# Sums of weight quarters for the seven products: from VectorE to accumulating DMAs

## Chip, cores and metric

The kernel runs on one core of one Trainium2 chip. The metric is the device time of one execution, in microseconds (us). Times come from one execution taken by the hardware profiler and from three timed runs.

## What is computed

One inference step of a backbone of two layers, on 640 tokens (128 context, 512 latent) of 1024 channels, in float32. Every layer is an FFN, a group of mixers (two attentions, a recurrence, a retention), and another FFN. The FFNs matter here; their hidden width is 2816, which is 22 chunks of 128:

```
def swiglu(h, wg, wu, wd):
    return (jax.nn.silu(h @ wg) * (h @ wu)) @ wd
...
  x += 1/2 * gate1 * SwiGLU_1(adaLN_1(RMSNorm(x)))
  x += gate2 * W_out [A | B | C | D](adaLN_2(RMSNorm(x)) @ W_in)
  x += 1/2 * gate3 * SwiGLU_2(adaLN_3(RMSNorm(x)))
```

## The kernel before

Channels lie on the 128 partitions, tokens along the free axis. Every float32 operand is split in two parts, high and low, and a product is made of three matmuls on TensorE (PE): high by high, high by low, low by high (`mm3`, L271 to L275). For weights, `parts` (L159) lets ScalarE (ACT) copy the high part (L168) and VectorE (DVE) subtract it for the low one (L169).

A hidden chunk needs a gate product and an up product. The first chunks of an FFN (`PLAIN`: 5, 4, 4 and 3 of the 22) are done plainly. The other 72 chunks of the four FFNs go through `strassen` (L593): the two weight blocks of a chunk, gate = [A11 | A12] and up = [A21 | A22], are taken as one 2 by 2 matrix of 512-column quarters, the activations as another one, and gate and up come out of seven products instead of eight (Winograd's form). A product is four `mm3`, so 12 matmuls of 320 columns, and a chunk is 84. Its accumulators are X, Y and Z in PSUM; `finish` (L602) copies or adds them after each product.

The seven weight operands are A11, S1 = A21 + A22, S2 = S1 - A11, S4 = A12 - S2, S3 = A11 - A21, A12 and A22. `seven` (L201) lists them as seven items. It loads gate and up whole (512 KB each); the four sums are made by DVE (L215, L219, L224, L228) in tiles named `ws`, and then split like any weight.

What sets the order: `take(ahead, deep)` (L177) hands out the next item to the program. When an item is used, those up to `AHEAD` = 2 items later are made (summed and split), and those up to `DEEP` = 7 further on are loaded. All loads are issued by SP, in that order, into a pool of 15 tiles of 128 x 1024 (`wide`) that loaded, summed and split weights share; a load waits until its tile is free. Each engine does its instructions in the order in which the program's scheduler put them. The 22 chunks are done in parts of four or three (`PARTS`, L17); after each part `down` (L678) multiplies the part's hidden chunks by eight weight tiles, one product of 24 or 18 matmuls each, and adds them to x on DVE (L682). Among the chunks of three of the four FFNs DVE also does rows of the modulation (L318, `mod_row`), with weights of 512 KB each. GpSimd (POOL) makes sums of the activations (`sums`, L460) before the first seven-product chunk of an FFN and small work of the mixers; it issues no DMA.

The sum S1, for example, is added before the split:

```
def s1():
    st["u"] = u = tiles.pop(r)
    st["s"] = wide("ws")
    V.tensor_add(st["s"][:, :512], u[:, :512], u[:, 512:])
    return parts(st["s"][:, :512], 512)
```

Of the kernel before, what the change touches and what calls it, by code (L numbers as in the profile page):

```python
# [53 lines left out]
def trunk(tc, A, O):  # L54
# [3 lines left out]
    with ExitStack() as es:  # L58
# [17 lines left out]
        def other():  # L76
            """the end of the stack of pools changes its form between the FFNs and the mixers"""
# [40 lines left out]
        # ---------------------------------------------------------------- constants, residual, conditions  # L118
# [18 lines left out]
        # ---------------------------------------------------------------- weights, prefetched in order  # L137
# [7 lines left out]
        def fetch(upto):  # L145
            while state["raw"] <= min(upto, len(raws) - 1):
                i = state["raw"]
                ap, n = raws[i]
# [6 lines left out]
                D.dma_start(out=dst, in_=ap)  # L155
                tiles[i] = raw
                state["raw"] += 1

        def parts(src, n):  # L159
            """the two parts of a float32 operand"""  # L160
# [6 lines left out]
            def go():  # L167
                S.activation(hi, src, AF.Copy)  # L168
# [8 lines left out]
        def take(ahead=2, deep=0):  # L177
            """the next weights; those of the next `ahead` items are made, the next `deep` of them loaded"""
# [10 lines left out]
        def plain(ap, n):  # L189
            raws.append((ap, n))  # L190
# [3 lines left out]
        def halved(ap, n):  # L194
            """a load of two items"""
            raws.append((ap, 2 * n))
# [4 lines left out]
        def seven(gate, up):  # L201
            """the weights of the seven products of one hidden chunk: gate = [A11 | A12], up = [A21 | A22]"""
            raws.append((gate, 1024))
            raws.append((up, 1024))
# [3 lines left out]
            def a11():  # L208
                st["g"] = tiles.pop(r - 1)
                return parts(st["g"][:, :512], 512)  # L210

            def s1():
                st["u"] = u = tiles.pop(r)
                st["s"] = wide("ws")
                V.tensor_add(st["s"][:, :512], u[:, :512], u[:, 512:])  # L215
                return parts(st["s"][:, :512], 512)

            def s2():
                V.tensor_sub(st["s"][:, 512:], st["s"][:, :512], st["g"][:, :512])  # L219
                return parts(st["s"][:, 512:], 512)  # L220

            def s4():
                st["s4"] = wide("ws")
                V.tensor_sub(st["s4"][:, :512], st["g"][:, 512:], st["s"][:, 512:])  # L224
                return parts(st["s4"][:, :512], 512)

            def s3():
                V.tensor_sub(st["s4"][:, 512:], st["g"][:, :512], st["u"][:, :512])  # L228
                return parts(st["s4"][:, 512:], 512)
# [26 lines left out]
        def ffn_units(l, w):  # L256
            for k0, k1 in PARTS:
                for f in range(k0, k1):
                    gu = [A["wgu"][l, w, f, i] for i in range(2)]
                    if f < PLAIN[l][w]:  # L260
                        for ap in gu:
                            plain(ap, 1024)
                    else:
                        seven(*gu)
# [6 lines left out]
        def mm3(out, wh, wl, xh, xl, first, last, more=False):  # L271
            """out (+)= w x, three products of their parts; `more` goes on with sums that were read already"""
# [11 lines left out]
        # ---------------------------------------------------------------- modulation  # L284
        # per (layer, group): tile [128, 2 conditions (latent, context), 8 chunks]
# [24 lines left out]
        def mod_row(l, g, k, c):  # L310
            """one condition's products for 128 columns of w_mod"""
# [417 lines left out]
        C = {}  # L729
# [793 lines left out]
```

## Time and profile before

| | |
|---|---|
| median of three runs | 2520.91 us (2519.56 to 2529.28) |
| profiled execution, span | 2521.9 us (the page gives no other time of it) |
| PE busy | 2467.4 us, 98% |
| DVE busy | 1974.8 us, 78% |
| ACT busy | 1141.8 us, 45% |
| POOL busy | 244.8 us, 10% |
| DMA | 261.88 MB, mean 104 GB/s |

An engine's busy time is the union of its instructions. A matmul is shown for some 310 ns but the next one begins 0.15 us after it, so that PE's pace is its busy time over the number of its matmuls. Idle time of an engine is put down to the instruction or DMA that ended it. The granted clock is that of PE; 1.00 is 2.4 GHz.

### The profile page before, as it was taken

To read this page: it belongs to the slowest core of one execution; us is meant where nothing else is said; L and a number is where in the kernel's file an instruction comes from. 1 tells how busy PE (TensorE), PEld (TensorE's weight loads), DVE (VectorE), ACT (ScalarE), POOL (GpSimd) and SP (SyncE) were. 2 spreads that over 40 slices of the span, in tenths; PEclk is the share of its full clock that TensorE was granted. 3 is DMA by queue.
4 is the path that set the end of the run, shared out by engine and by line. 5 is a ranking of instruction groups with operands and counts; after the bars stand their busy time and mean duration, and the time that the engine had idled before them with its cause. 6 is when DMAs were issued, how large, how long until landed. Compare 5 with 4: busy or idle time off the path is not lost.

```text
span 2521.9 us, 43865 instructions
## 1 busy us (share of the span) xinstructions
PE 2467.4 (98%) x17376; PEld 2365.6 (94%) x17376; DVE 1974.8 (78%) x3850; ACT 1141.8 (45%) x2271; POOL 244.8 (10%) x251
## 2 busy tenths in 40 slices
PE   7999999999999999999999999999999999999999
PEld 6999999996888999999999999999878789999999
DVE  6899989856666898988989898897656668666765
ACT  5344334563345633443463344344634556433433
POOL 2100000022420200000020000000433102000000
PEclk9999999999999999999999999999999999999999
DMA  7544344222102244443424444342110022222222
GB/s 253 185 152 138 127 129 148 94 78 67 37 18 66 93 144 134 143 133 118 141 89 148 134 142 133 119 134 78 58 60 26 18 76 76 77 67 81 87 81 71
DMA packets 92303, 261.88 MB, mean 104 GB/s; under 512 B 10049, under 2 KB 20929, under 8 KB 92097
## 3 DMA queue, kind: packets, MB, share of 16 engines
q1 hardware_dynamic: 92096, 259.07, 31.7%
q8 instruction: 137, 2.24, 0.4%
q14 instruction: 70, 0.57, 0.1%
HBM read 255.63 MB, written 3.41 MB: 103 GB/s over the span
## 4 chain that ended last, share of the span: by engine, by line
PE 67%; DVE 4%; ACT 2%; POOL 1%; issue 1%; DVEq 0%; POOLq 0%; ACTq 0%
PE dn L273 8%; PE dn L274 7%; PE dn L275 7%; PE x L274 5%; PE x L275 5%; PE x L273 5%; PE y L274 3%; PE y L275 3%; PE y L273 3%; PE pt L1290 2%; PE ao L1299 2%; PE g L274 2%; PE g L273 2%; PE g L275 1%; PE z L273 1%; PE z L274 1%
## 5 line engine op out<-in xcount | busy, mean ns | idle before, releaser
L273 PE MATMUL dn<-hidh,wp 128*128 128x320 f32 x1408 | 434.5, 311 | 0.0
L275 PE MATMUL dn<-hidh,wp 128*128 128x320 f32 x1408 | 433.9, 309 | 0.0
L274 PE MATMUL dn<-hidl,wp 128*128 128x320 f32 x1408 | 433.7, 309 | 0.2 <-DVE hidl L281 0.2
L168 ACT ACTIVATE wp<-ws 128x512 fp32r<-128x512 f32 x288 | 180.8, 630 | 393.2 <-DVE ws L215 149.9
L168 ACT ACTIVATE wp<-raw 128x512 fp32r<-128x512 f32 (+1 forms) x408 | 243.7, 611 | 212.1 <-DVE wp L169 84.2
L682 DVE SCALAR_TENSOR_TENSOR x<-dn,mod,x 128x128 f32<-128x128 f32 (+3 forms) x488 | 233.8, 518 | 126.4 <-PE dn L275 125.3
L318 DVE SCALAR_TENSOR_TENSOR junk<-wm,cond 128x1024 bf16<-128x1024 f32 x256 | 304.5, 1218 | 4.6 <-DMA wm<-in_wmod 4.5
L169 DVE TENSOR_TENSOR wp<-raw,wp 128x512 fp32r<-128x512 f32 (+1 forms) x408 | 266.2, 667 | 51.9 <-ACT wp L168 47.0
L273 PEld LDWEIGHTS dn<-hidh,wp 128*128 128x128 f32 x1408 | 264.5, 188 | 4.8 <-ACT hidh L280 3.7
L274 PEld LDWEIGHTS dn<-hidl,wp 128*128 128x128 f32 x1408 | 264.8, 188 | 0.6 <-DVE hidl L281 0.6
L275 PEld LDWEIGHTS dn<-hidh,wp 128*128 128x128 f32 x1408 | 264.6, 188 | 0.0
L169 DVE TENSOR_TENSOR wp<-ws,wp 128x512 fp32r<-128x512 f32 x288 | 197.4, 691 | 17.6 <-ACT wp L168 17.0
L274 PE MATMUL g<-hl,whi 128*128 128x320 f32 x608 | 192.6, 318 | 3.2 <-DVE hl L528 1.7
L275 PE MATMUL g<-hh,wlo 128*128 128x320 f32 x608 | 190.5, 314 | 0.0
L273 PE MATMUL g<-hh,whi 128*128 128x320 f32 x608 | 185.5, 318 | 4.5 <-ACT hh L527 2.2
L273 PE MATMUL x<-hh,wp 128*128 128x320 f32 x576 | 178.3, 310 | 1.0 <-DVE sl L613 1.0
L274 PE MATMUL x<-hl,wp 128*128 128x320 f32 x576 | 178.5, 310 | 0.0
L275 PE MATMUL x<-hh,wp 128*128 128x320 f32 x576 | 178.3, 309 | 0.0
L169 DVE TENSOR_TENSOR wlo<-raw,whi 128x1024 fp32r<-128x1024 f32 x88 | 109.8, 1249 | 61.2 <-ACT whi L168 46.0
L425 POOL TENSOR_TENSOR nrs<-nrm,neghalf 80x4 f32<-80x4 f32 x12 | 13.3, 1106 | 1377.1 <-DVE nrm L423 1377.1
L168 ACT ACTIVATE whi<-raw 128x1024 fp32r<-128x1024 f32 x88 | 92.5, 1052 | 80.5 <-PE dk L274 20.7
L274 PEld LDWEIGHTS g<-hl,whi 128*128 128x128 f32 x608 | 117.1, 193 | 5.9 <-DVE hl L454 3.5
(331 smaller groups left out, 6655.2 us busy)
## 6 DMA issues: line engine op xcount, KB each, us to landing
raw<-in_wgu SPq DMA_DIRECT2D x176, 512.0 KB, 3.5
wm<-in_wmod SPq DMA_DIRECT2D x128, 512.0 KB, 4.0
raw<-in_wd SPq DMA_DIRECT2D x64, 512.0 KB, 3.8
raw<-in_wd SPq DMA_DIRECT2D x32, 384.0 KB, 3.4
raw<-in_wint SPq DMA_DIRECT2D x20, 512.0 KB, 3.5
wm<-in_wm SPq DMA_DIRECT2D x32, 256.0 KB, 5.5
raw<-in_wqkv SPq DMA_DIRECT2D x16, 512.0 KB, 3.5
raw<-in_wocd SPq DMA_DIRECT2D x8, 512.0 KB, 3.4
```

What stands on the lines that cost most here:

```text
L168: S.activation(hi, src, AF.Copy)
L169: V.tensor_sub(lo, src, hi.bitcast(F32))
L273: PE.matmul(out, wh, xh, start=first, stop=False, skip_group_check=more)
L274: PE.matmul(out, wh, xl, start=False, stop=False, skip_group_check=more)
L275: mark["pe"] = PE.matmul(out, wl, xh, start=False, stop=last, skip_group_check=more)
L318: V.scalar_tensor_tensor(junk, modraw["w"], 1.0, cond[c], OP.mult, OP.mult, accum_out=modraw[(l, g)][:, c, k:k + 1])
L425: G.tensor_tensor(r, s, neghalf[:80, :4], op=OP.pow)
L682: V.scalar_tensor_tensor(x[d][:, s0:s1], pv[:, s0 - base:s1 - base], gate[:, c, d:d + 1], x[d][:, s0:s1], OP.mult, OP.add)
L1290: PE.transpose(p[:, c0 - a0:c0 - a0 + 128], P[:, c0:c0 + 128], idn)
L1299: PE.matmul(o[kv * 64:kv * 64 + 64, :128], vs[i][:, kv * 64:kv * 64 + 64], pts[kv][:, i * 128:i * 128 + 128], start=i == 0, stop=i == nb - 1)
```

## The change

Three sums come from DMAs that add what they read to what the tile holds, issued by POOL. The tile z is loaded as [A11 | A21], and `up` = [A21 | A22] is accumulated on it, so that it holds [A11 + A21 | A21 + A22]. Its right half is S1 with the sign turned; A11 is then accumulated on it (S2 turned), and A12 (S4). Each accumulation waits until the split of the sum before has read the half. So `up` stands with its sign turned in all seven products: S3 = A11 + A21, S1 = -(A21 + A22), S2 = S1 - A11, S4 = A12 - S2. `parts` has a form that splits the negative of its source. A22 is loaded by itself. The up half of a hidden chunk comes out negative; one sum of the activations (L475) changes its sign, the plain chunks take a factor -1 (L665), and the FFN's gate is multiplied by -0.5 instead of 0.5 (L389 of before). The products run in the order X, Y, X, Z, X, Y, X instead of X, Y, X, Y, X, Z, X, and the steps of `finish` move with them.

```
 def fetch(upto):
...
                 D.dma_start(out=dst, in_=ap)
+                if add is not None:
+                    G.dma_start(out=raw[:, :n], in_=add, accum_op=OP.add)
...
+        def parts(src, n, neg=False):
...
+                if neg:
+                    S.activation(hi, src, AF.Copy, scale=-1.0)
+                    V.scalar_tensor_tensor(lo, src, -1.0, hi.bitcast(F32), OP.mult, OP.subtract)
+                    return
...
+        def seven(gu):
+            gate, up = gu[0], gu[1]
+            raws.append((gate, 1024, None))
+            raws.append((gu[:, :, :512].rearrange("i p n -> p i n"), 1024, up))
+            raws.append((up[:, 512:], 512, None))
             r = len(raws) - 1
             st = {}
 
             def a11():
-                st["g"] = tiles.pop(r - 1)
+                st["z"] = z = tiles.pop(r - 1)
+                st["s1"] = parts(z[:, 512:], 512, True)
+                G.dma_start(out=z[:, 512:], in_=gate[:, :512], accum_op=OP.add)
+                st["g"] = tiles.pop(r - 2)
                 return parts(st["g"][:, :512], 512)
...
             def s2():
-                V.tensor_sub(st["s"][:, 512:], st["s"][:, :512], st["g"][:, :512])
-                return parts(st["s"][:, 512:], 512)
+                z = st["z"]
+                p = parts(z[:, 512:], 512, True)
+                G.dma_start(out=z[:, 512:], in_=gate[:, 512:], accum_op=OP.add)
+                return p
...
-            for make in (s1, s2, s4, s3, lambda: parts(st["g"][:, 512:], 512), lambda: parts(st["u"][:, 512:], 512)):
+            for make in (lambda: st.pop("s1"), s2, lambda: parts(st["g"][:, 512:], 512), lambda: parts(st["z"][:, :512], 512),
+                         lambda: parts(st["z"][:, 512:], 512), lambda: parts(tiles.pop(r)[:, :512], 512)):
                 items.append((r, make))
...
-                V.tensor_scalar(o[:, :, k0:k1], o[:, :, k0:k1], 0.5, None, OP.mult)
+                V.tensor_scalar(o[:, :, k0:k1], o[:, :, k0:k1], -0.5, None, OP.mult)
...
-                E1.tensor_sub(t4[:, 320:], hi[:, :320], t[:, 320:])
+                E1.tensor_sub(t4[:, 320:], t[:, 320:], hi[:, :320])
...
                     elif i == 3:
+                        V.tensor_add(ct[:, one], ct[:, one], Z)
+                        S.activation(ct[:, one], ct[:, one], AF.Silu)
+                    elif i == 4:
+                        V.tensor_add(sl[:, two], sl[:, one], X)
+                    elif i == 5:
                         V.tensor_add(ct[:, two], ct[:, two], Y)
                         S.activation(ct[:, two], ct[:, two], AF.Silu)
-                    elif i == 4:
-                        V.tensor_add(sl[:, two], sl[:, one], X)
                         V.tensor_mul(sl[:, two], sl[:, two], ct[:, two])
...
-                for i, (o, b, new) in enumerate(((X, "11", True), (Y, "t1", True), (X, "t2", False), (Y, "22", False),
-                                                 (X, "t3", False), (Z, "21", True), (X, "t4", False))):
+                for i, (o, b, new) in enumerate(((X, "11", True), (Y, "t1", True), (X, "t2", False), (Z, "21", True),
+                                                 (X, "t3", False), (Y, "22", False), (X, "t4", False))):
...
-                    V.tensor_mul(sl, sl, uv)
+                    V.scalar_tensor_tensor(sl, uv, -1.0, sl, OP.mult, OP.mult)
```

The diff also drops comments and moves line numbers by a few: L168 and L169 are L174 and L175 after the change, the negative form is L171 and L172, and the accumulations are L157 (`up` on z), L220 (A11) and L227 (A12).

What stands on DVE before, in the fourth chunk of a part of the first layer's second FFN (raw_17152 is the gate, raw_17173 is up, `wp` the split weights, `junk` the modulation):

```order
L215 TENSOR_TENSOR ws_17308<-raw_17173 128x512
L219 TENSOR_TENSOR ws_17308<-ws_17308,raw_17152 128x512
L281 TENSOR_TENSOR hidl_17191<-sl_17058,hidh_17190 128x640
L169 TENSOR_TENSOR wp_17310<-ws_17308,wp_17310 128x512
L318 SCALAR_TENSOR_TENSOR junk_17256,modraw_16973<-wm_17254,cond_14257 128x1024
L318 SCALAR_TENSOR_TENSOR junk_17313,modraw_16973<-wm_17254,cond_14260 128x1024
L169 TENSOR_TENSOR wp_17338<-ws_17308,wp_17338 128x512
L224 TENSOR_TENSOR ws_17356<-raw_17152,ws_17308 128x512
L228 TENSOR_TENSOR ws_17356<-raw_17152,raw_17173 128x512
```

The same chunk on DVE after the change (raw_17115 is z, raw_17113 the gate; wp_17245 is S1, wp_17293 is S2, wp_17346 is S4):

```order
L172 SCALAR_TENSOR_TENSOR wp_17245<-raw_17115,wp_17245 128x512
L280 TENSOR_TENSOR hidl_17151<-sl_17019,hidh_17150 128x640
L175 TENSOR_TENSOR wp_17249<-raw_17113,wp_17249 128x512
L317 SCALAR_TENSOR_TENSOR junk_17213,modraw_16932<-wm_17211,cond_14222 128x1024
L317 SCALAR_TENSOR_TENSOR junk_17269,modraw_16932<-wm_17211,cond_14225 128x1024
L172 SCALAR_TENSOR_TENSOR wp_17293<-raw_17115,wp_17293 128x512
L175 TENSOR_TENSOR wp_17312<-raw_17113,wp_17312 128x512
L609 TENSOR_TENSOR ct_17157<-ct_17157,z_17156 128x320
L175 TENSOR_TENSOR wp_17328<-raw_17115,wp_17328 128x512
L612 TENSOR_TENSOR sl_17158<-sl_17158,x_17154 128x320
L175 TENSOR_TENSOR wp_17346<-raw_17115,wp_17346 128x512
```

The four sums are gone; between the splits of S1, S2 and S4, each of which reads what a DMA has written since the last, stand the other splits, two rows of the modulation and sums from PSUM.

On POOL nothing stood in these chunks before. After the change, around the third (raw_16976) and fourth chunk (raw_17115) of the same part:

```order
L157 DMA raw_16976<-in_wgu 128x1024
L227 DMA raw_16807<-in_wgu 128x512
L220 DMA raw_16976<-in_wgu 128x512
L157 DMA raw_17115<-in_wgu 128x1024
L227 DMA raw_16976<-in_wgu 128x512
L220 DMA raw_17115<-in_wgu 128x512
L227 DMA raw_17115<-in_wgu 128x512
```

The first accumulation of a chunk comes between the second and the third of the chunk before.

## Rows read from the trace of the kernel before

**Rows 1.** The page's first part: busy time, share, instructions by engine.
```profile
span 2521.9 us, 43865 instructions
...
PE 2467.4 (98%) x17376; PEld 2365.6 (94%) x17376; DVE 1974.8 (78%) x3850; ACT 1141.8 (45%) x2271; POOL 244.8 (10%) x251
```

**Rows 2.** Busy time by engine in the seven-product stretches of the four FFNs.
```profile
core 0: us, PE busy (x) PEld busy (x) DVE busy (x) ACT busy (x) POOL busy (x), PEclk, DMA share, GB/s
140.00:460.00 320.00, 319.05 (x2170) 317.71 (x2169) 295.25 (x573) 138.35 (x259) 2.90 (x1) 1.00 0.43 140
860.00:1240.00 380.00, 379.52 (x2571) 377.83 (x2569) 341.21 (x598) 157.92 (x291) 11.58 (x11) 1.00 0.42 135
1300.00:1680.00 380.00, 379.50 (x2575) 377.90 (x2575) 338.58 (x597) 157.62 (x294) 12.02 (x12) 1.00 0.41 133
2110.00:2500.00 390.00, 389.52 (x2648) 387.94 (x2647) 266.99 (x464) 164.92 (x307) 0.78 (x1) 1.00 0.25 76
sum 1470.00, PE 1467.59 PEld 1461.38 DVE 1242.03 ACT 618.81 POOL 27.28; mean PE 366.90 PEld 365.34 DVE 310.51 ACT 154.70 POOL 6.82
```

**Rows 3.** PE's waits over the whole span: us in total, times, longest.
```profile
PE nsum L421 <- DVE sq L412: 13.1, 1, 13.1
PE ro L1073 <- DVE pm L1067: 8.7, 2, 4.4
...
PE x L273 <- DVE sl L613: 1.0, 2, 0.6
```

**Rows 4.** Groups of DVE instructions by shape: count, busy us, mean ns, idle before.
```profile
L169 DVE TENSOR_TENSOR wp<-ws,wp 128x512 fp32r<-128x512 f32 x288 | 197.4, 691 | 17.6 <-ACT wp L168 17.0
...
L219 DVE TENSOR_TENSOR ws<-ws,raw 128x512 f32<-128x512 f32 x72 | 50.1, 696 | 1.0
L215 DVE TENSOR_TENSOR ws<-raw 128x512 f32<-128x512 f32 x72 | 49.9, 692 | 0.7 <-PE x L275 0.7
L224 DVE TENSOR_TENSOR ws<-raw,ws 128x512 f32<-128x512 f32 x72 | 49.4, 686 | 1.4 <-PE x L275 0.3
L228 DVE TENSOR_TENSOR ws<-raw 128x512 f32<-128x512 f32 x72 | 49.3, 684 | 0.0
...
L616 DVE TENSOR_TENSOR ct<-ct,z 128x320 f32<-128x320 f32 x72 | 34.8, 483 | 4.2 <-PE z L275 3.6
...
L665 DVE TENSOR_TENSOR sl<-sl,g 128x640 f32<-128x640 f32 x16 | 13.0, 815 | 8.8 <-PE g L275 6.7 <-ACT sl L664 2.0
```

**Rows 5.** The group of ACT's high parts of the sums.
```profile
L168 ACT ACTIVATE wp<-ws 128x512 fp32r<-128x512 f32 x288 | 180.8, 630 | 393.2 <-DVE ws L215 149.9 <-PE dn L275 82.8 <-DVE ws L224 54.9
```

**Rows 6.** DMA queues (share of 16 engines) and issues (median us to landing).
```profile
q1 hardware_dynamic: 92096, 259.07, 31.7%
...
raw<-in_wgu SPq DMA_DIRECT2D x176, 512.0 KB, 3.5
...
wm<-in_wm SPq DMA_DIRECT2D x32, 256.0 KB, 5.5
...
ck<-in_ck SPq DMA_DIRECT2D x2, 256.0 KB, 4.0
cv<-in_cv SPq DMA_DIRECT2D x2, 256.0 KB, 2.8
```

**Rows 7.** The groups of POOL instructions: a small tensor operation and the cheapest.
```profile
L425 POOL TENSOR_TENSOR nrs<-nrm,neghalf 80x4 f32<-80x4 f32 x12 | 13.3, 1106 | 1377.1 <-DVE nrm L423 1377.1
...
L880 POOL MEMSET xp<- 128x3 f32 x4 | 0.4, 96 | 0.0
```

**Rows 8.** The tile raw on SP: ns of an issue, and all its landings.
```profile
L155 SPq DMA_DIRECT2D raw<-in_wgu x176: 327/328/1055, 11.4 to 2456.7; - x176
...
DMA to landing us min/median/max: 3.1/3.6/8.3
```

**Rows 9.** Timeline of PE in a mixer: start us, us, instruction, idle time before it.
```profile
585.57 0.74 PE L1073 MATMUL ro<-pm,dvn 128*64 128x512 f32 x1 [4.39 <-DVE pm L1067]
```

**Rows 10.** Busy time by engine just behind that wait, columns as in rows 2.
```profile
586.00:589.40 3.40, 3.40 (x9) 1.62 (x8) 2.54 (x7) 0.00 (x0) 0.94 (x2) 0.50 0.00 0
```

More of the change, by code (lines that the diff above doesn't have):

```diff
@@ L147, in fetch @@
                 i = state["raw"]
-                ap, n = raws[i]
+                ap, n, add = raws[i]
                 raw = wide("raw")
@@ L155, in fetch @@
                 D.dma_start(out=dst, in_=ap)
+                if add is not None:
+                    G.dma_start(out=raw[:, :n], in_=add, accum_op=OP.add)
                 tiles[i] = raw
                 state["raw"] += 1
-        def parts(src, n):
+        def parts(src, n, neg=False):
             if n <= 512:
@@ L189, in plain @@
         def plain(ap, n):
-            raws.append((ap, n))
+            raws.append((ap, n, None))
             r = len(raws) - 1
@@ L194, in halved @@
         def halved(ap, n):
-            raws.append((ap, 2 * n))
+            raws.append((ap, 2 * n, None))
             r = len(raws) - 1
@@ L199, in halved @@
             items.append((r, lambda: parts(tiles.pop(r)[:, n:2 * n], n)))
-        def seven(gate, up):
-            raws.append((gate, 1024))
-            raws.append((up, 1024))
+        def seven(gu):
[3 more added lines that the diff above has]
+            raws.append((up[:, 512:], 512, None))
             r = len(raws) - 1
@@ L258, in ffn_units @@
                 for f in range(k0, k1):
-                    gu = [A["wgu"][l, w, f, i] for i in range(2)]
                     if f < PLAIN[l][w]:
-                        for ap in gu:
-                            plain(ap, 1024)
+                        for i in range(2):
+                            plain(A["wgu"][l, w, f, i], 1024)
                     else:
-                        seven(*gu)
+                        seven(A["wgu"][l, w, f])
                 n = (k1 - k0) * 128
@@ L609, in finish @@
                     elif i == 3:
+                        V.tensor_add(ct[:, one], ct[:, one], Z)
[3 more added lines that the diff above has]
+                    elif i == 5:
                         V.tensor_add(ct[:, two], ct[:, two], Y)
                         S.activation(ct[:, two], ct[:, two], AF.Silu)
-                    elif i == 4:
-                        V.tensor_add(sl[:, two], sl[:, one], X)
                         V.tensor_mul(sl[:, two], sl[:, two], ct[:, two])
-                    elif i == 5:
-                        V.tensor_add(ct[:, one], ct[:, one], Z)
-                        S.activation(ct[:, one], ct[:, one], AF.Silu)
                     else:
                         V.tensor_mul(sl[:, one], ct[:, one], X)
-                for i, (o, b, new) in enumerate(((X, "11", True), (Y, "t1", True), (X, "t2", False), (Y, "22", False),
-                                                 (X, "t3", False), (Z, "21", True), (X, "t4", False))):
+                for i, (o, b, new) in enumerate(((X, "11", True), (Y, "t1", True), (X, "t2", False), (Z, "21", True),
+                                                 (X, "t3", False), (Y, "22", False), (X, "t4", False))):
                     wh, wl = take(AHEAD, DEEP)
```

12 lines of the change are left out of this document (removed).

## Prediction

> **What bounds the kernel now.** The page's first part comes first: TensorE (PE) is busy in 98% of the span, VectorE (DVE) in 78% [rows 1]. A mean over unlike stages says little, so I then read the stretches of the four FFNs in which the seven-product chunks and their down products run [rows 2]. PE is busy there in 1467.6 of 1470.0 us; DVE fills 89 to 92% of the first three stretches and 68% of the last. The page counts 16 DMA engines as 0.25 to 0.43 busy there. Last, the waits of PE [rows 3]: its long ones are at the start and in the mixers. Of those that name the seven products, the waits for the DVE sum of L613 come to 1.0 us in all. So PE's own work sets the time, DVE is nearly as full but never late, and what DVE is relieved of has no path into the end. All that the change can give in these stretches is 1470.0 - 1467.6 = 2.4 us.
>
> The pace: 2571 matmuls in 379.5 us of PE are 0.148 us each [rows 2], a product (12 matmuls) is 1.77 us, a chunk (84) some 12.35 us. Four chunks are followed by eight down products of 24 matmuls, 28 us.
>
> **What the change removes.** Four DVE sums of each of 72 chunks, at 0.68 to 0.70 us [rows 4]: 288 x 0.69 = 198 us of DVE, one tenth of its busy time. On the path they are worth nothing, by the 2.4 us above. Two low parts of each chunk become three-operand operations with a sign; that they cost as much as the two-operand ones (0.69 us) is my assumption, and the same holds for the 16 products that take a -1; both stay beneath PE's work, with 2.4 us of DVE freed in each chunk as cover. The turned sums and the factor -0.5 cost nothing: as many instructions as before. The reordered products are the same 84 matmuls; the Y accumulator is read for the last time in product 5 instead of 3, which leaves product 6 and the next chunk's first, 3.5 us, before Y is written again, against one DVE sum of 0.48 us, a row that [rows 4] gives for the same shape. No PE time from that.
>
> **What it adds.** Per chunk a plain load of 256 KB and three accumulating DMAs, 512 + 256 + 256 KB, all issued by POOL, and they form a chain: load z, add `up` on it, split S1 off, add A11, split S2 off, add A12, split S4. Before, the two loads are issued far ahead, so that only SP's queue waits for buffers; a DVE sum of 0.69 us stood between S1 and S2. Now a whole DMA stands there, and another between S2 and S4. PE does not see it directly: what waits is ACT's copy of the high part and DVE's subtraction (L171, L172), both in order on their engines. Queued behind them are the PSUM copies and sums of the chunk in work (L603 to L618) and the splits of the next products; PE waits for those. POOL's own other work in these stretches is nearly nothing [rows 2].
>
> **The room for the chain.** On DVE, from the S1 split of one chunk to that of the next, these cannot overlap with either DMA: three low parts (S1, S2, S4) of 0.69 us, the two high parts of S2 and S4 on ACT of 0.63 us that stand between a landing and its low part [rows 5], one PSUM product (L618, 0.48 us) and the last quarter's low part (0.69 us) [rows 4]: 2.07 + 1.26 + 1.17 = 4.5 us. With chunks following each other every 12.35 us, both DMAs together may take 12.35 - 4.5 = 7.8 us, 3.9 us each, counted from the end of DVE's subtraction to the start of ACT's copy. While they fly, the order lets DVE do the hidden chunk's split, one low part and two rows of the modulation in the first gap, and four PSUM steps and two low parts in the second, so up to that size nothing is lost.
>
> **The price of one accumulating DMA.** No row of before shows one, nor a DMA issued by POOL. Nearest rows: plain loads of 256 KB by SP land after 2.8 us (cv), 4.0 us (ck) and 5.5 us (wm, in the crowded start) [rows 6]. The hardware queue moved 259.07 MB in 31.7% of 16 engines' 2521.9 us, which is 20.25 GB/s per engine [rows 6]: 256 KB over 16 engines are 0.8 us. An accumulation has to fetch the old sum too; nothing to 0.8 us more, and I take 0.8. POOL makes the issue: between its cheapest row, 0.1 us, and a small tensor operation of 1.1 us [rows 7]; SP's issue is 0.33 us [rows 8]. I take the upper one, since a description of 128 rows is more than a memset. So 2.8 + 0.8 + 1.1 = 4.7 us; ends 2.9 us and 5.5 + 0.8 + 1.1 = 7.4 us. The upper half has a reason in the rows: a chunk's DMA work rises from 2 x 1.6 = 3.2 us to 1.25 MB plain (4.0 us) and 1 MB twice (6.5 us), in a cycle of 12.35 + 7 us with its share of the down products. That is 0.38 more of the DMA engines on top of 0.41 to 0.43 [rows 2], and loads that land in 3.6 us at the median have taken 8.3 us even now [rows 8].
>
> The Trainium skill ("Collectives: The Full Stack", The bandwidth ceiling) says that an add in a DMA needs two source reads and measured about half a copy's rate; no run here shows it yet. By it the 0.8 us stays; without it the DMA is 3.9 us, just at its room.
>
> The first accumulation (512 KB) is off this path: z is fetched nine products (15.9 us) before its chunk's first, and load 3.5 + (3.5 + 1.6 + 1.1) + split 1.3 = 11.0 us.
>
> **The sum.** At 4.7 us each, a chunk's chain is 2 x 4.7 - 7.8 = 1.6 us longer than PE's chunk. It adds up over the chunks of one part; two products made ahead (3.5 us) absorb the first of it, and the 28 us of down products, which have no such chain, restore them. The 72 chunks lie in 11 parts of four, 9 of three and 1 of one. A part of four loses 4 x 1.6 - 3.5 = 2.9 us, one of three 3 x 1.6 - 3.5 = 1.3 us: 31.9 + 11.7 = 43.6 us. The gain of at most 2.4 us I leave out. 2521.9 + 43.6 = 2565.5 us in the profiled execution, whose span is 1.0 us over the median of the three runs: 2564.5 us.
>
> **Rivals.**
> Hidden after all. Two accumulations of up to 4.3 us each leave at most 0.9 us per chunk, which the products made ahead absorb: PE stays at its 99.8% and the time is 2519 to 2526 us. It decides at 4.3 to 4.4 us. For it: the plain load's 2.8 us, and an overlapped second read. Against: POOL's issue has to fit in 1.5 us with everything else. The Trainium skill ("DMA: Bandwidth & Descriptors", Anatomy of one DMA — SWDGE (gpsimd) path) gives a DMA from POOL about 2.0 us and its bytes at 436 GB/s; that would be 2.6 us for 256 KB, and this rival. The rows of plain loads (2.8 to 5.5 us) are all above that.
>
> Crowded queue. At 5.6 us each (the wm row without surcharge, or the chosen one with the data term doubled by other loads), a chunk lacks 3.4 us: 11 x 10.1 + 9 x 6.7 = 171 us, 2692 us. At 7.4 us, 2950 us. Waits of that size cost PE's clock too: after a wait of 4.39 us the granted clock was 0.50 for 3.4 us, at 1.2 GHz instead of 2.4 [rows 9, 10], so up to 1.7 us more for each of 20 parts.
>
> Faster. DVE at 90% might brake PE in ways that its waits do not show, as longer matmuls. The pace is 147.0, 147.6, 147.4 and 147.1 ns in the four stretches [rows 2]; the last has the least DVE work and no modulation, yet is no better than the first. At most 5000 matmuls by 0.6 ns, 3 us, with the 2.4 us: 2515 us. That is still inside half a per cent.
>
> **How the numbers follow.** A measurement of this kernel can tell about 0.5%, 12.6 us, from no change. Chain too long by a little to 7%: 0.43. Hidden (all within 0.5%): 0.40, with a few us of loss still counted here. Crowded beyond 7%: 0.13. Faster by more: 0.04. So slower 0.56, same 0.40, faster 0.04. The forecast is that of the first case, 2564.5 us; by itself it spans 2534 to 2692. The range must take in the hidden case, down to 2515, and ends at 2692, leaving out the crowded end.
>
> **What would show it.** Right: PE waits in the four stretches that name L603 to L618 copies or split weights, ACT's or DVE's waits for a DMA on L171 to L175, an accumulation of 4.4 us or more, losses at the third and fourth chunk of a part and none in down products; the last FFN, whose engines are at 0.25, suffers least. DVE busy falls by some 198 us in any case, and bytes rise by 1.25 MB x 72 = 94 MB. Wrong: PE still at 99.8% there with accumulations under 4 us; or losses that begin at POOL (an accumulation queued behind that of the next chunk, whose load is late) rather than at the landing.

## The result and the profile after

The changed kernel takes 2753.98 us (2750.96 to 2756.23, 4 runs) against 2523.36 us before on the same chip: a ratio of 1.0907 (95% interval 1.0887 to 1.0928). It is 230 us slower; the prediction was 2564.5 us with a range up to 2692, so the direction was right, but the time lies above the range and the predicted loss is a fifth of the real one.

The page's first part, queues and DMA issues after; they answer to [rows 1] and [rows 6]:

```profile
span 2754.3 us, 44397 instructions
...
PE 2532.4 (92%) x17376; PEld 2411.3 (88%) x17376; DVE 1810.5 (66%) x3562; ACT 1126.7 (41%) x2271; POOL 432.8 (16%) x467
...
q1 hardware_dynamic: 111680, 277.95, 30.8%
q0 software_dynamic: 31104, 75.51, 16.7%
...
HBM read 350.00 MB, written 3.41 MB: 128 GB/s over the span
...
raw<-in_wgu SPq DMA_DIRECT2D x176, 512.0 KB, 4.4
...
raw<-in_wgu POOLq DMA_DIRECT2D x72, 512.0 KB, 6.4
raw<-in_wgu POOLq DMA_DIRECT2D x144, 256.0 KB, 5.0
```

PE does the same 17376 matmuls but is busy 65.0 us longer, and it is idle for the rest of the loss, 167 us. The POOL queue is new: an accumulation of 256 KB takes 5.0 us from its issue to its landing, one of 512 KB 6.4 us. DVE is relieved of its sums and is now at 66%.

PE's waits after (total us, times, longest), beside [rows 3], where the waits on the seven products came to 1.0 us:

```profile
PE x L272 <- ACT ct L603: 101.1, 37, 7.5
PE x L272 <- DVE sl L612: 34.3, 22, 2.8
PE x L272 <- ACT ct L607: 18.1, 11, 3.1
...
PE g L272 <- ACT sl L663: 10.8, 2, 9.1
```

These four are 164.3 us. None of them is a wait for weights. L603, L607 and L612 are the steps of `finish` that free the accumulator X after products 0, 2 and 4.

One such wait, from the timeline of the kernel after: the second chunk of a part in the second FFN begins at 1208.8 us (columns: start us, us, engine, line, operation, tiles; in brackets the idle time before and what ended it). `wp<-raw` at 1213.81 is the split of an S4, which waits for the accumulation that POOL issued at 1206.17:

```profile
1205.63 0.86 POOL L157 DMA_DIRECT2D raw<-in_wgu  x1 [6.47 <-DMA raw<-in_wgu]
...
1206.17 1.22 POOL L227 DMA_DIRECT2D raw<-in_wgu  x1
...
1208.84 0.49 DVE L616 TENSOR_TENSOR sl<-sl,ct 128x320 f32<-128x320 f32 x1 [0.54 <-ACT ct L615]
...
1213.81 1.15 ACT L174 ACTIVATE wp<-raw 128x512 fp32r<-128x512 f32 x2 [5.00 <-DMA raw<-in_wgu]
...
1214.47 0.69 DVE L175 TENSOR_TENSOR wp<-raw,wp 128x512 fp32r<-128x512 f32 x1 [5.14 <-ACT wp L174]
...
1215.08 0.48 DVE L618 TENSOR_TENSOR sl<-ct,x 128x320 f32<-128x320 f32 x1
...
1215.73 0.72 ACT L279 ACTIVATE hidh<-sl 128x640 fp32r<-128x640 f32 x1
...
1216.88 0.42 ACT L603 ACTIVATE ct<-x 128x320 f32<-128x320 f32 x1
```

ACT and DVE stand idle for 5 us until that split can start. Queued behind it on DVE is L618, the last sum of the chunk that is just over; on ACT behind that, L279, and then L603, the copy of the new chunk's first product. PE had finished that product at 1210.6 and wants X again for the third. Its row, and the window just behind it (columns as in rows 2):

```profile
1217.35 0.64 PE L272 MATMUL x<-t12h,wp 128*128 128x320 f32 x1 [4.81 <-ACT ct L603]
```

```profile
1217.10:1220.40 3.30, 3.05 (x11) 3.06 (x12) 3.29 (x6) 0.52 (x2) 1.69 (x2) 0.50 0.57 81
```

The granted clock is 0.50 after the wait, 1.2 GHz instead of 2.4: the wait is paid for a second time in slow matmuls. Over the program the trace has PE busy at this level for 135.7 us, against 34.7 us before. Matmuls take about twice as long there (11 in 3.05 us above, against 0.15 us each), so half of the 101 us more, some 50 of the 65.0 us, is what the lower clock cost (an estimate). Most of the rest can be the way that busy time is counted: PE pauses for over 0.1 us 123 times instead of 50, and the last matmul ahead of a pause counts with its 310 ns and not with the pace of 150 ns (an estimate: 73 x 0.16 = 12 us).

The four FFNs after (columns and counterpart: [rows 2]; other stretches, as the program is longer):

```profile
140.00:550.00 410.00, 346.37 (x2187) 340.01 (x2186) 271.64 (x529) 142.25 (x270) 46.52 (x50) 0.93 0.64 165
1010.00:1400.00 390.00, 353.81 (x2291) 347.73 (x2290) 258.22 (x467) 143.78 (x273) 43.36 (x50) 0.96 0.67 171
1500.00:1890.00 390.00, 353.57 (x2298) 347.50 (x2298) 261.58 (x472) 142.12 (x272) 45.10 (x52) 0.97 0.66 171
2320.00:2730.00 410.00, 386.74 (x2567) 380.94 (x2567) 213.07 (x379) 156.05 (x297) 47.27 (x54) 0.99 0.55 129
```

Where in a part the loss sits, from the starts of the matmuls: mean time of a chunk, from its first matmul to the start of what follows its seventh product, and the sum of what exceeds 12.35 us.

```
chunk of its part         1st    2nd    3rd    4th
before, mean us         12.37  12.38  12.35  12.33
after, mean us          14.70  18.20  14.31  13.59
after, excess us         49.4  117.0   39.3   13.7
```

### The profile page after: what moved, and what is told of

The parts are those of the page before. It is cut to its first block, busy times and chain, and to the rows that moved or that the text cites. A ratio compares the mean times of both kernels' runs of the same rounds, so it can differ in the third digit from the quotient of the medians.

```text
span 2754.3 us, 44397 instructions
## 1 busy us (share of the span) xinstructions
PE 2532.4 (92%) x17376; PEld 2411.3 (88%) x17376; DVE 1810.5 (66%) x3562; ACT 1126.7 (41%) x2271; POOL 432.8 (16%) x467
## 3 DMA queue, kind: packets, MB, share of 16 engines
q0 software_dynamic: 31104, 75.51, 16.7%
## 5 line engine op out<-in xcount | busy, mean ns | idle before, releaser
L175 DVE TENSOR_TENSOR wp<-raw,wp 128x512 fp32r<-128x512 f32 (+1 forms) x552 | 377.6, 688 | 254.2 <-ACT wp L174 250.8
L174 ACT ACTIVATE wp<-raw 128x512 fp32r<-128x512 f32 (+1 forms) x552 | 331.2, 613 | 461.6 <-DMA raw<-in_wgu 189.7
L171 ACT ACTIVATE wp<-raw 128x512 fp32r<-128x512 f32 x144 | 90.7, 630 | 378.4 <-DMA raw<-in_wgu 206.4
L272 PE MATMUL x<-hh,wp 128*128 128x320 f32 x576 | 182.9, 318 | 35.0 <-DVE sl L612 34.3
L272 PE MATMUL g<-hh,whi 128*128 128x320 f32 x608 | 186.9, 320 | 13.7 <-ACT sl L663 10.8
L272 PE MATMUL x<-t12h,wp 128*128 128x320 f32 x288 | 102.8, 357 | 101.2 <-ACT ct L603 101.1
L172 DVE SCALAR_TENSOR_TENSOR wp<-raw,wp 128x512 fp32r<-128x512 f32 x144 | 99.1, 688 | 141.7 <-ACT wp L171 141.6
L274 PE MATMUL x<-hh,wp 128*128 128x320 f32 x576 | 180.1, 313 | 0.0
L220 POOL DMA_DIRECT2D raw<-in_wgu x72 | 63.0, 876 | 648.0 <-DVE wp L172 594.1
L272 PEld LDWEIGHTS x<-t12h,wp 128*128 128x128 f32 x288 | 61.4, 213 | 111.6 <-ACT ct L603 111.5
L157 POOL DMA_DIRECT2D raw<-in_wgu x72 | 64.0, 889 | 578.4 <-DMA raw<-in_wgu 365.9
```

The costliest lines, as they stand in the source:

```text
L157: G.dma_start(out=raw[:, :n], in_=add, accum_op=OP.add)
L171: S.activation(hi, src, AF.Copy, scale=-1.0)
L172: V.scalar_tensor_tensor(lo, src, -1.0, hi.bitcast(F32), OP.mult, OP.subtract)
L175: V.tensor_sub(lo, src, hi.bitcast(F32))
L220: G.dma_start(out=z[:, 512:], in_=gate[:, :512], accum_op=OP.add)
L272: PE.matmul(out, wh, xh, start=first, stop=False, skip_group_check=more)
```

## Experiments: which part of the change

**Order and signs alone.** The new order of products, the turned signs and the three-operand splits, with all four sums still made by DVE.

```diff
-                G.dma_start(out=z[:, 512:], in_=gate[:, :512], accum_op=OP.add)
...
+                V.tensor_add(st["s"][:, 512:], st["s"][:, :512], st["g"][:, :512])
+                return parts(st["s"][:, 512:], 512, True)
```

> Signs turned and products in the new order, as in the changed kernel, but the four sums by VectorE (with the new signs) and loads as before: no accumulating DMA. Theory A (the chain of two accumulations inside a chunk holds ACT and DVE, which are in order, and PE waits for their PSUM copies) and theory B (the added DMA traffic makes every load late) both expect the time of before: 2510 to 2535 us, PE over 99.5% busy in the FFN stretches. Theory C (the order of the products or the signed three-operand splits cost something themselves) expects over 2560 us.

2527.35 us, ratio 1.0017 (1.0003 to 1.0031). The order and the signs cost about 0.2%; the loss comes with the DMAs.

**The first accumulation alone** (`up` on z, 512 KB; S2 and S4 by DVE).

```diff
-                G.dma_start(out=z[:, 512:], in_=gate[:, :512], accum_op=OP.add)
...
+                V.tensor_add(st["s"][:, :512], st["z"][:, 512:], st["g"][:, :512])
```

> Of the three accumulations of a chunk only the first is left (up on z, 512 KB, fetched nine products ahead); S2 and S4 are summed by VectorE. Half of the accumulated bytes and the whole extra plain load stay; the chain inside the chunk is gone. A: the first accumulation has 15.9 us of lead and needs some 12 (load 4.4, issue and landing 6.4, split 1.3), so 2515 to 2545 us. B: about half to two thirds of the 230 us loss stays, 2630 to 2680 us.

2557.54 us, ratio 1.0135 (1.0110 to 1.0159): 34 us, between the two ranges. Not free, but a seventh of the loss. PE's longest waits on the seven products here, and those of its down products:

```profile
PE x L272 <- ACT ct L603: 20.1, 12, 5.9
...
PE dn L272 <- ACT hidh L279: 3.9, 4, 1.5
```

**The chain of two alone** (the two accumulations of 256 KB; S1 and S3 by DVE, loads as before).

```diff
-            raws.append((gu[:, :, :512].rearrange("i p n -> p i n"), 1024, up))
+            raws.append((up, 1024, None))
...
+                V.tensor_add(z[:, 512:], u[:, :512], u[:, 512:])
```

> The other half: S1 and S3 summed by VectorE, loads as before (two of 512 KB), and the two 256 KB accumulations for S2 and S4 as in the changed kernel. A: the chain stays, but the 512 KB accumulation that POOL issues between them is gone. In the trace of the changed kernel S4's accumulation took 8.2 us where it stood right behind that one, S2's 6.4 us. If both fall to 5 us the chain is 2 x 5 - 7.8 = 2.2 us too long per chunk, 2580 to 2650 us; if the 512 KB one has no part in it, 2720 to 2760 us. B: half of the added bytes, 2620 to 2650 us; B alone cannot be told from A here, but by e2 it can.

2734.76 us, ratio 1.0841 (1.0807 to 1.0874). With half the accumulated bytes, and with no 512 KB accumulation in POOL's queue, it makes 213 of the 230 us.

**The 512 KB accumulation moved**: issued by POOL behind the last one of the chunk before, so that it can't stand in front of it as at 1205.63 above.

```diff
+                with tc.issue_after(G.dma_start(out=z[:, 512:], in_=gate[:, 512:], accum_op=OP.add).ins):
+                    flush()
```

> The changed kernel with one order turned: on POOL the next chunk's 512 KB accumulation stands behind this chunk's last one instead of ahead of it. All bytes and all waits stay. A with the collision as a main part: S4's wait falls from about 8 to 5.5 us, 2 us for most chunks in the middle of a part, 2620 to 2700 us. A without it, and B: 2730 to 2770 us. It may also get worse, if the 512 KB accumulation now comes too late for S1 (over 2790 us).

2783.42 us, ratio 1.1029 (1.1004 to 1.1054). The 256 KB ones land faster now (4.3 us at the median instead of 5.0), yet the time is longer, and in none of the ranges. S1 comes later: ACT's splits wait 55.8 us for the 512 KB ones (31 times), against 4.4 us (4 times) in the changed kernel. So this run alone does not settle what the collision of DMAs costs; the chain alone, which has no such collision and loses 213 us, shows that it is not the main cause.

## Experiments: what the chain costs, and why

The chain alone is the base of the next runs: it is shorter to follow, and its accumulations land in 4.3 us at the median.

**Writes instead of additions.** S2 and S4 are then not the sums.

```diff
-                G.dma_start(out=z[:, 512:], in_=gate[:, :512], accum_op=OP.add)
+                G.dma_start(out=z[:, 512:], in_=gate[:, :512])
```

> The chain of two with plain writes instead of accumulations: the same DMAs from POOL, of the same size, in the same places, but each overwrites its target and does not add (S2 and S4 are therefore not the sums; the rest of the work is all there). It tells what the second read of an addition is worth. Theory Q: the chain's time is paid twice per chunk, so every 1 us by which a write lands before an accumulation (4.3 us at the median) takes about 2 us from each of some 50 to 70 chunks, 100 to 140 us; if a write lands 0.8 us earlier, as the second read was estimated in the prediction, 80 to 110 us of the 213 us go: 2625 to 2655 us. If a write lands no earlier, nothing goes: 2735 us. Theory T (the traffic in the DMA engines slows everything): the share of the second read in the bytes, 37.7 MB of some 300, would be worth little: 2700 us or more.

2605.59 us, ratio 1.0325 (1.0302 to 1.0348). From the page of that run, and then from the page of the chain alone:

```profile
q0 software_dynamic: 11520, 37.76, 4.4%
...
ws<-in_wgu POOLq DMA_DIRECT2D x144, 256.0 KB, 3.1
```

```profile
q0 software_dynamic: 20736, 37.76, 8.9%
...
ws<-in_wgu POOLq DMA_DIRECT2D x144, 256.0 KB, 4.3
```

The same bytes take the DMA engines half the time when they are not added, and land 1.2 us sooner, not 0.8. That takes 129 us off the loss, 108 us for each us of landing, as theory Q has it; 144 DMAs by 1.2 us are 173 us, so three quarters of what the landings became shorter by had stood on the path. The run changes the landing and the load of the DMA engines together; the runs with other places, below, tell them apart.

**One accumulation per chunk** (S2; S4 by DVE).

```diff
-                G.dma_start(out=z[:, 512:], in_=gate[:, 512:], accum_op=OP.add)
...
+                V.tensor_add(z[:, 512:], st["g"][:, 512:], z[:, 512:])
```

> The chain of two without its second link: S2 is still made by an accumulating DMA of 256 KB, S4 by a DVE sum again (72 accumulations instead of 144, no other change against the kernel with the chain alone, 2734.8 us). Theory Q (queues): the lost time comes from a ring of steps in order on ACT and DVE: S1's split, accumulation, S2's split, accumulation, S4's split, the PSUM steps of the chunk in work, the next S1. In the trace of the chain alone S1 to S1 took 17.7 us at the median against the 12.35 us that TensorE needs for a chunk; without the second accumulation (4.3 us to land, 1.65 us from S2's copy to its issue) and with a DVE sum (0.7 us) it is about 12.5 us: no more than 10 to 40 us of the 213 us stay, 2530 to 2562 us. Theory E (each accumulation costs a fixed amount, by its traffic or by a stall of its own): half of 213 us stay, 2628 us.

2631.57 us, ratio 1.0420 (1.0394 to 1.0445): 108 us, half, which is theory E's value. Theory Q fails here as it stood, with a ring whose length alone decides: by its sum one accumulation leaves the ring as long as PE's chunk, and it still costs 1.5 us per chunk. That it is no fixed price of a DMA, as theory E has it, is shown by the runs below, where the same DMAs cost much less. The ACT timeline of this run shows how one wait costs, and PE's next wait (line numbers are 3 higher in this kernel):

```profile
1083.66 0.44 ACT L608 ACTIVATE sl<-y 128x320 f32<-128x320 f32 x1 [0.76 <-PE y L277]
1087.91 0.63 ACT L171 ACTIVATE wp<-ws 128x512 fp32r<-128x512 f32 x1 [3.81 <-DMA ws<-in_wgu]
1088.45 0.42 ACT L610 ACTIVATE ct<-x 128x320 f32<-128x320 f32 x1
```

```profile
1088.92 0.41 PE L275 MATMUL x<-t3h,wp 128*128 128x320 f32 x1 [1.79 <-ACT ct L610]
```

The split of S2 waits for its DMA, and the copy of the third product (L610, L607 above) is queued behind it. A single wait at that place costs, however much room the chunk has as a whole. In the chunk before, the copy stood ahead of the split (1071.67 and 1074.08 us), and it was the next step for X, DVE's sum of the fifth product behind the low part, that came late.

**Other places in the queues.** Instructions and DMAs as in the chain alone; only their order on ACT and DVE is changed. First, S1's split behind L605, S2's behind L615 and L616, S4's behind L607 of its own chunk:

```diff
+            with ExitStack() as st:
+                for m in behind.get(name, ()):
+                    st.enter_context(tc.issue_after(m.ins))
...
-                    elif i == 1:
-                        S.activation(sl[:, one], Y, AF.Copy)
+                    elif i == 1:
+                        behind["s1"] = [S.activation(sl[:, one], Y, AF.Copy)]
```

> The chain of two with nothing changed but places in the queues: the split of S1 stands on ACT and DVE behind the PSUM copy of the second product of the chunk in work, that of S2 behind the last two steps of its sixth product, that of S4 behind the copy of the third product of its own chunk. The same instructions, the same DMAs; the splits come later, nearer to the products that use them. Theory Q: the PSUM steps no longer stand behind waits for a DMA, and the ring shrinks to 1.65 + 4.3 + 1.65 + 4.3 + 0.6 = 12.5 us, since S4's split and the next S1's are now neighbours: loss of 10 to 100 us, 2530 to 2620 us. Theory W (weights late: the split weights themselves reach TensorE too late because a chain of DMAs is long): all splits of the sums come later still, so it gets worse than 2734.8 us.

2681.60 us, ratio 1.0628 (1.0599 to 1.0657). Better by 53 us, not by the 115 to 205 expected. S4's split now stands ahead of the next chunk's S1, so that the next chain starts when this one has ended. Theory W has a part here: 26 us of PE's waits name split weights, against 0.4 us in the chain alone. Then the same with S1's split ahead of that S4, which for this is made only when its product takes it:

```diff
+            if name == "s1" and "s4" in behind:
+                behind["s4"].append(state["high"])
...
+            return got() if callable(got) else got
...
+                         lambda: lambda: queued("s4", st["z"][:, 512:], 512), lambda: parts(st["u"][:, 512:], 512)):
```

> As the run with the splits behind the PSUM steps, and S1's split of the next chunk now stands ahead of S4's split of this one. Then no split waits in a ring with the next chunk's: S2's has some 5.8 us from the issue of its accumulation to its own place, S4's some 5.3 us, and S1's waits for neither. Theory Q: accumulations that land in 4.3 us are hidden but for the late ones; 2522 to 2565 us, and fewer than 30 us of TensorE's waits name the copies of the first and third product. Theory W: worse than 2734.8 us. Theory E or T: 2735 us, as the DMAs and their bytes are the same.

2550.86 us, ratio 1.0102 (1.0072 to 1.0132). Of 213 us 27 are left, with the same DMAs landing in the same 4.3 us, and only 2.0 us of PE's waits name the copy of the first product (fewer than 30 expected). Putting the splits behind the PSUM steps gave back 53 us, and cutting the ring another 131. One stretch of the second FFN in the chain alone and in this run (columns as in rows 2):

```profile
920.00:1260.00 340.00, 322.30 (x2131) 317.97 (x2130) 259.99 (x459) 125.88 (x234) 33.93 (x37) 0.98 0.52 148
```

```profile
920.00:1260.00 340.00, 339.18 (x2310) 338.27 (x2310) 275.31 (x503) 133.18 (x257) 30.65 (x35) 1.00 0.57 154
```

More matmuls in the same time, at a higher DMA share. And the split of S2 on ACT in this run, which no longer waits (L182; L627 is L615 above):

```profile
1032.74 0.47 ACT L627 ACTIVATE ct<-ct 128x320 f32<-128x320 f32 x1 [2.61 <-DVE ct L626]
1033.12 0.62 ACT L182 ACTIVATE wp<-ws 128x512 fp32r<-128x512 f32 x1
```

**One accumulation, its split behind L615 and L616.**

> The run with one accumulation per chunk (2631.6 us), with S2's split put behind the last steps of the sixth product on ACT and DVE. Theory P (a single wait costs by its place: there, S2's copy waited 3.8 us for the accumulation on ACT with the copy of the third product behind it, and TensorE lost 1.9 us at the fifth product): with the place changed the 108 us go nearly all, 2522 to 2540 us. Theory R (only the length of a ring of steps counts, which is 12.5 us with one accumulation whatever the places): no change, 2620 to 2640 us.

2567.27 us, ratio 1.0166 (1.0143 to 1.0188). 108 us became 42, between the two ranges: the place decides, but less went than expected. In the second and third FFN nothing is left (table below). Most of what PE still waits for on the seven products is the copy of the next chunk's first product (L614, L603 above), which is the urgent step behind the new place when the DMA lands late:

```profile
PE x L283 <- ACT ct L614: 13.0, 11, 3.1
```

**The whole changed kernel with the three places.**

> The whole changed kernel (2754.0 us), all three accumulating DMAs with their sizes and sources, with nothing changed but the places of the splits on ACT and DVE: S1's behind the copy of the second product of the chunk in work, S2's behind the last steps of the sixth, S4's behind the copy of the third product of its own chunk and behind the next S1. Theory Q (waits for a DMA standing ahead of PSUM steps in the in-order queues): as the chain alone went from 2734.8 to 2550.9 us by that, most of the 231 us go here too, and the first accumulation (512 KB, 6.4 us to land, which alone cost 34 us) still makes S1 late at some chunks: 2550 to 2610 us. Theory T (bytes and the DMA queue): with 512 KB more per chunk, read twice, loads and accumulations delay each other, and the loss stays over 120 us: 2645 us or more.

2568.76 us, ratio 1.0175 (1.0151 to 1.0200). 230 us became 44, with the three accumulations, their bytes and sources untouched. What is left of the copies' waits (L615 and L619 are L603 and L607 above):

```profile
PE x L284 <- ACT ct L615: 13.2, 8, 6.2
...
PE x L284 <- ACT ct L619: 4.7, 6, 1.4
```

**The first accumulation alone, S1's split behind L605.**

> The run with the first accumulation alone (512 KB, 2557.5 us), with S1's split put behind the copy of the second product of the chunk in work. Theory P: its 34 us came from the same cause, S1's split waiting on ACT for the accumulation with the copy of the first product behind it; 2522 to 2540 us. Theory L (the 256 KB of extra loads and the double reads delay the loads themselves): 2550 us or more.

2552.04 us, ratio 1.0112 (1.0093 to 1.0131). Only 34 to 28 us, theory L's value; but PE's waits do not name loads (L287 and L611 are L279 and L603 above):

```profile
PE dn L280 <- ACT hidh L287: 8.7, 6, 3.2
...
PE x L280 <- ACT ct L611: 8.4, 2, 6.2
```

The waits for the first product's copy fell from 20.1 to 8.4 us, as theory P has it. In their stead the down products wait longer, 8.7 us instead of 3.9, for the last hidden chunk of their part, whose steps stand on ACT behind the split of the next S1 and its wait. The two waits that are left are in the first two seven-product chunks of the program, which take 20.7 and 16.3 us, 12 us more than two of 12.35. The longer one, 6.2 us, is no wait for a DMA: the copy stands on ACT behind the last plain chunk's hidden split, that one waits for DVE, and DVE is at work on sums of activations and small operations of the mixers, without a pause since it waited 4.2 and 1.3 us for POOL's part of these, some 20 us earlier. The first chunk takes 20.7 to 21.7 us in every run with the first accumulation and 12.3 to 15.2 us in all others.

## Experiments: what is left

**The places alone**, with S2 and S4 by DVE.

> The places of the splits as in the run with the chain apart (2550.9 us), but S2 and S4 made by DVE sums: no accumulating DMA at all. It tells how much of that run's 27 us is the later place of the splits and how much is left of the DMAs. If the DMAs are fully hidden: 2545 to 2555 us here too. If the places are free: 2520 to 2530 us, and the 27 us are accumulations that land late.

2532.33 us, ratio 1.0035 (1.0022 to 1.0048): a third of a per cent, of which the order and the signs had about 0.2% (ratio 1.0017) already without the later places.

**The traffic alone**: the places, sums by DVE, and the two accumulations into a tile that nobody reads.

```diff
+            G.tensor_copy(unread[i][:, :1], split[1][:, :1].bitcast(F32))
+            G.dma_start(out=unread[i], in_=src, accum_op=OP.add)
```

> The kernel with the places alone (2532.3 us, sums by DVE) plus the two accumulating DMAs of 256 KB per chunk at the points where the chain issues them, into a tile that no computation reads (the outputs do not depend on them; POOL copies one column of the split into that tile ahead of each, so that it is issued in time). The same bytes and POOL issues as with the chain apart (2550.9 us), but no split waits. Theory P (waits): traffic costs nothing, 2527 to 2538 us, and the chain apart's 18 us over the places alone are accumulations that land late. Theory T (traffic): 2545 to 2556 us, as with the chain apart.

2566.99 us, ratio 1.0168 (1.0142 to 1.0193), the value of neither theory. PE waited in the mixers, most likely since the tile had taken one of their work tiles:

```profile
PE dk L294 <- DVE qdb L1016: 39.0, 2, 19.5
```

In the next run the tile is taken for each chunk only.

> The traffic run with one difference: the tile that nobody reads is a work tile taken for each chunk (and cleared by POOL), not one kept for the whole program, so that the mixers have all their 41 work tiles again. Theory P (waits, not traffic): 2527 to 2540 us, as the places alone (2532.3 us). Theory T: 2550 us or more, with the loss in the FFN stretches.

2544.94 us, ratio 1.0077 (1.0051 to 1.0103): 0.4% over the places alone, between the two ranges, and the wait in the mixers is gone. So of the chain apart's 1.0% the order, the signs and the places have some 0.35, the traffic and POOL's extra work another 0.4, though no split waits for them, and 0.25 are left for accumulations that land late, which is within the scatter of these runs. In the stretch above the traffic costs nothing:

```profile
920.00:1260.00 340.00, 340.00 (x2308) 338.77 (x2307) 294.61 (x537) 130.21 (x253) 52.98 (x87) 1.00 0.54 152
```

The time from an FFN's first matmul into y or z to its last down product shows where each run loses (the second and the third FFN follow each other and stand together):

```
us                                 first   second + third   last
before                             339.1        791.9      388.3
after                              426.2        897.6      418.3
chain alone                        400.0        892.9      425.9
first accumulation                 355.9        806.9      391.7
one accumulation                   382.4        833.4      405.1
one accumulation, split behind     365.1        792.3      391.9
chain, splits behind               377.6        853.8      435.1
chain apart                        355.7        793.9      389.5
whole change, places               363.1        810.8      388.4
first accumulation, split behind   355.8        794.4      398.9
places alone                       346.2        792.0      386.7
traffic alone, tile per chunk      351.2        791.9      387.7
```

With the places, accumulations of 256 KB are hidden in the second and third FFN to within 2 us of 792. What they still cost is mostly in the first, which begins just behind the program's start. The landings there are no longer (4.4 us at the median for S2's, in the first FFN as in the second, with the chain apart). Why it is there, beyond the first chunk's wait above, and why all three together keep 19 us in the second and third, was not told apart further.

## Why the prediction was wrong, by its steps

**The removed sums are worth nothing on the path; order and signs are free.** Right for the order and the signs: 0.2% with these alone, and the splits with a sign take 688 ns, as the plain ones. No run takes the sums away without putting DMAs in, so that they are worth nothing rests on [rows 2] and [rows 3]. DVE's busy time fell by 164.3 us, not 198; the sums' rows are gone, but a DVE instruction starts a little before the one ahead of it has ended (1214.47 + 0.69 against 1215.08), so sums taken out of a dense row free less than their own durations. The durations themselves fell by 188.7 us, so this makes 24 of the 34 us.

**The price of an accumulation.** Right, in part by luck: taken as 4.7 us; measured 4.3 us in the chain alone and 5.0 us in the whole change. Its parts were off in both directions and cancel: 0.87 us for POOL's issue (1.1), 1.2 us for the addition (0.8), which leaves 2.2 us for the rest (2.8). The bytes, predicted as 94 MB more, are 350.00 - 255.63 = 94.4 MB. The forecast's doubt between 0.8 us and nothing for the second read is settled: on q0 an engine moved 75.51 MB / (0.167 x 16 x 2754.3 us) = 10.3 GB/s, on q1 20.5. The Trainium skill ("Collectives: The Full Stack", The bandwidth ceiling) puts a collective's add, with its two source reads, at about half a copy's rate; the trace agrees, with 10.3 against 20.5 GB/s for a DMA into SBUF. The Trainium skill ("DMA: Bandwidth & Descriptors", Anatomy of one DMA — SWDGE (gpsimd) path) has about 2.0 us plus the bytes at 436 GB/s for a DMA from POOL, an estimate of 2.6 us here; the plain write took 3.1 us and the accumulation 4.3, and the measured times decide.

**The room for the chain: the step that failed.** The prediction let a chunk lose only what its chain exceeds 12.35 us by, with 7.8 us of room for two DMAs, and nothing below that. With the measured price (4.3 us, and 0.3 us from DVE's subtraction to the issue) that is 2 x 4.6 - 7.8 = 1.4 us per chunk, 11 x 2.1 + 9 x 0.7 = 29 us for the chain alone, which lost 213; with 5.3 us in the whole change 129 us, which lost 230; and nothing for one accumulation, which lost 108. The sum compared lengths, where the places in the queues decide. The prediction names ACT and DVE as in order and L603 to L618 as queued behind the splits, and then says that other work fills the gaps "so up to that size nothing is lost". It never asked when each step in the queue behind a wait is due: X is freed by L603, L607 and L612 with one product, 1.77 us, to spare, while a split may wait up to 5 us. The length was too small as well: in the chain alone one S1 follows the other after 17.7 us at the median, where 4.5 us and twice 4.6 make 13.7. From the landing of S4's DMA to the next chunk's first issue alone it is 6.1 us at the median (as from 1596.23 to 1602.33 us), as S4's split, PSUM steps and the next S1's split stand behind each other there. Both parts show in the runs: of 213 us the places behind the PSUM steps gave back 53, and letting the next S1 go ahead of S4 another 131.

**Two products made ahead absorb 3.5 us.** Wrong in an instructive way. Splits are made far earlier than that: in the chain alone S4's was copied at 1596.31 us and used at 1608.25 us. PE had its weights 12 us ahead and waited all the same. A lead in an in-order queue is no stock: the early split, waiting for its DMA, stands in front of a copy that is due now. Moving the splits later, which the rival theory of late weights would have punished, took away most of the loss.

**The first accumulation is off the path.** Wrong by 34 us. PE waits 12 times for the first product's copy, 20.1 us in all; the longest of these waits, 5.9 us, is in the program's first chunk and not for the DMA.

**PE's clock.** Only a rival had it, with up to 1.7 us per part, 34 us. PE's busy time grew by 65.0 us for the same matmuls, and some 50 us of that, a fifth of the loss, are the lower clock.

**What was to show it.** Right: waits that name L603 to L612, ACT's and DVE's waits for DMA on the splits, next to none in the down products (1.9 us), the last FFN least. Wrong: the third and fourth chunks. The second loses most (117.0 us), as the table shows, and the fourth least. One of the signs of being wrong came true in part: the loss begins at POOL too, where an accumulation of 256 KB is issued right behind one of 512 KB (1205.63 and 1206.17 us, landing after 7.6 us instead of 5.0). That is so in 8 of the 72 chunks, and the run that turned that order became slower.

**The cases.** The time, 9.1% longer, falls in the case beyond 7%, which had a chance of 0.13, but not for its reason: "Crowded queue" has 5.6 us for an accumulation and 2692 us, and the accumulations were cheaper than that. The range ended where the price ended, and no rival had a cost of the wait's place.

## What to carry to other kernels

Before an operation is replaced by a DMA that an in-order engine waits for, list what stands behind that wait in the engine's queue and when each of those instructions is due; the shortest of these margins, and not only the room in the whole loop, is what the DMA may take. If it must stay, put the waiting instruction behind the urgent ones, and the start of the next chain ahead of the end of this one. An engine that is nearly full but never late (here DVE at 78%) has nothing to give.

## What the runs showed of the hardware

An addition in a DMA doubles the time of its bytes on the DMA engines (8.9% against 4.4% for the same 37.76 MB) and lands 256 KB after 4.3 us instead of 3.1. POOL's issue takes 0.87 us, against 0.33 us of SP's [rows 8]. After a wait of 4.81 us TensorE ran at 1.2 GHz for the 3.3 us shown; over the program PE was busy at that level for 135.7 us, against 34.7 us before.
